# A hybrid attention/convolution block on one NeuronCore: x loaded in smaller first parts, its squares later, the warm-up on a zeroed tile, the transposes of q and k two half chunks later

## The chip, the cores and the metric

The kernel runs on one core of a Trainium2 chip. The metric is the device time of one execution in microseconds; the time before is the median of three runs. A profiled execution gives the trace that is read here; its clock starts at the program's first instruction, and its span ends with the last.

## What is computed

One layer for 256 tokens of width 2048, in float32 (the parts that matter here):

```python
xn = rms_norm(h, norm1_g[l])
proj = jnp.einsum('bsd,dn->bsn', xn, w_in[l])
q, k, v, ga, gg = jnp.split(proj, ...)
q = apply_rope(rms_norm(q, q_norm_g[l]), cos, sin)
k = apply_rope(rms_norm(k, k_norm_g[l]), cos, sin)
att = diff_attention(q, k, v, lam)          # 4 heads, block-causal mask
att = rms_norm(att, subln_g[l]) * (1.0 - lambda_init)
u = ga * jax.nn.sigmoid(gg)
u = causal_depthwise_conv(u, conv_w[l], conv_b[l])   # 31 taps
u = jax.nn.silu(layer_norm(u, conv_ln_g[l], conv_ln_b[l]))
h = h + jnp.einsum('bsm,md->bsd', jnp.concatenate([att, u], axis=-1), w_out[l])
hn = rms_norm(h, norm2_g[l])
a, bu = hn @ w_gate[l], hn @ w_up[l]
h = h + (jax.nn.silu(a) * bu) @ w_down[l]
```

## The kernel before

**Products in three passes.** Each operand of a large product is split into a high part (a cast, on ACT) and a low part (the rest, on DVE), and a product is high times high, low times high and high times low. The weights come in *chunks* of two 128-row tiles by 512 columns (512 KB). Of each chunk, `load_chunk` issues the transfer on SP (L315), `round_chunk` casts `whi` on ACT (L320), `split_chunk` makes `wlo` on DVE (L329), and `multiply` runs twelve matmuls: eight that read `whi` (L359, L360), then four that read `wlo` (L365). Five buffers hold raw chunks, three hold each of `whi` and `wlo`.

**The order is written out by hand.** `run_chunks` walks through the chunks. For chunk t it first issues the load, cast and split of chunk t+2 (t+1 in the opening, the first nine chunks), then chunk t's matmuls. All other work hangs on generators in the list `running`: `resume()` is called twice a chunk, after the first eight matmuls and after the last four, and lets each generator go on to its next `yield`. `lag(n)` waits for n such half chunks, `room` for free banks among the four `aux` banks of PSUM. What a generator issues goes into the engines' queues at that place, and each engine works through its queue in this order. Between these steps `run_side` gives DVE taps of the convolution (L517), as many as a credit allows.

**The opening.** A warm-up of 17 transposes of the identity matrix (L157) stands ahead of everything on PE; the identity and a small constant come from POOL. x arrives transposed, in parts: `XLOADS` says ahead of which chunk which of its 16 tiles are loaded (L433, into the buffers of q's and k's later transposes, `qT` and `kT`). `x_split` scales and casts each tile on ACT (L233) and makes the low part on DVE (L234). Chunks 0 and 1 hold one tile each, chunks 2 to 8 two. `x_norm` squares x in place in four parts of four tiles on ACT (L443), adds them on DVE (L445, L455), and sums over the partitions on PE (L460). It is started ahead of chunk 0, squares a part once its tiles are split, and one part a half chunk at most.

**The blocks of 512 columns.** The columns of `w_in` run in ten blocks: four of the convolution's gates (the first has nine chunks, the others eight), then k, q, k, q, then v twice. `qk_done` starts `qk_rows` for each half of the tokens (row 0, row 1), two half chunks apart. `qk_rows` sums squares on ACT (L427), takes the root on POOL (L217, L218, L615), after `LAG[0]` half chunks scales on ACT (L619), after `LAG[1]` rotates on DVE (L626 to L629), after `LAG[2]` transposes four tiles on PE (L634) and copies them on ACT (L635). When all rows of a k and a q block are there, `attend_scores` starts for two heads, four half chunks apart: scores on PE (L649), maxima on DVE (L657, L659), exponentials on ACT (L668), reciprocals on DVE and a factor on POOL (L677, L679), scaling on ACT (L688), sum on DVE (L695), transposes on PE (L701 to L703), copy on ACT (L706). `v_done` copies v on ACT (L712) and starts `attend_values` (PE L727), which waits for the copy of L706 and ends in transposes (L746) and the split of the result, from which the output projection reads. After that come the output projection, the gated feed-forward layer and the rest, which take the time from about 300 us to the end.

Of the kernel before, what the change touches and what calls it, by code (L numbers as in the profile page):

```python
# [12 lines left out]
F32 = mybir.dt.float32  # L13
# [5 lines left out]
P = 128  # L19
# [12 lines left out]
N = 512  # L32
# [17 lines left out]

WARM = 17

XLOADS = {0: range(0, 1), 1: range(1, 4), 3: range(4, 8), 5: range(8, 12), 7: range(12, 16)}
XSQUARES = 4

XWHOLE = 40
# [7 lines left out]
RAW_BUFS = 5  # L64
AUX = 4

LAG = (3, 2, 6)
HL_BUFS = 3

KTILE_US = 1.30  # L70
# [52 lines left out]
def tile_block(  # L123
# [6 lines left out]
    act, dve, pool, pe, sp = nc.scalar, nc.vector, nc.gpsimd, nc.tensor, nc.sync  # L130
# [8 lines left out]
    small = prestack.enter_context(tc.tile_pool(name="small", bufs=4))  # L139
    acc_ps = ctx.enter_context(tc.tile_pool(name="acc", bufs=4, space=PSUM))  # L140
    aux_ps = ctx.enter_context(tc.tile_pool(name="aux", bufs=AUX, space=PSUM))
# [3 lines left out]
    away = ctx.enter_context(tc.tile_pool(name="away", bufs=1, space=bass.MemoryType.DRAM))  # L145
    hd = [away.tile([P, D], F32, tag=f"hd{m}", name=f"hd{m}") for m in range(NM)]

    ident = const.tile([P, P], F32, tag="ident", name="ident")
    make_identity(nc, ident)
    neghalf = const.tile([P, 8], F32, tag="neghalf", name="neghalf")  # L150
    pool.memset(neghalf, -0.5)


    def warm_up(n):
        warm = aux_ps.tile([P, N], F32, tag="aux", name="ps_warm")
        for _ in range(n):
            pe.transpose(warm[:, :P], ident, ident)  # L157

    warm_up(WARM)

    cols = const.tile([P, NR], F32, tag="cols", name="cols")
    act.dma_start(out=cols, in_=gains)
# [78 lines left out]
    def start(gen):  # L241
        running.append(gen)
# [7 lines left out]
    def lag(n):  # L250
        for _ in range(n):
            yield
# [4 lines left out]
    def room(n, hold=0):  # L257
        while held[0] + n > AUX:
            yield
        held[0] += hold  # L260
# [170 lines left out]
    def x_load(ks):  # L431
        half = qkT["qk"[ks[0] // 8]]
        sp.dma_start(out=half[:, ks[0] % 8 : ks[-1] % 8 + 1, :], in_=xt[:, ks[0] : ks[-1] + 1, :])  # L433

    def x_split(ks):
        for k in ks:
            xT[k] = lhs_pair("x", k)
            split_scaled(xT[k], qkT["qk"[k // 8]][:, k % 8, :], col("g1", k))
# [8 lines left out]
    def x_norm():  # L447
        for n in range(KD // XSQUARES):
            while len(xT) < (n + 1) * XSQUARES:
                yield  # L450
            x_square(n)
            yield
        sq = qkT["q"]
        for w in (2, 1):
            dve.tensor_tensor(sq[:, :w, :], sq[:, :w, :], sq[:, w : 2 * w, :], ALU.add)  # L455
        yield from lag(2)
        yield from room(1)
        ps = aux_ps.tile([P, N], F32, tag="aux", name="ps_n")
        for m in range(NM):
            pe.matmul(ps[:, m : m + 1], sq[:, 0, m * P : (m + 1) * P], neghalf[:, :1], start=True, stop=True)  # L460
        yield
        ss = small.tile([P, NM], F32, tag="ss1", name="ss1")
        act.copy(ss, ps[:, :NM])
        for m in range(NM):
            rsqrt_mean(rstd1[m], ss[:, m : m + 1], -D / 2, EPS)
        yield
        normed.append(True)
# [138 lines left out]
    def qk_rows(key, b, m, ps):  # L606
# [8 lines left out]
        pool.tensor_scalar(f, f, rstd1[m], 0.0, ALU.mult, ALU.add)  # L615
        yield from lag(LAG[0])
        qn = pre.tile([P, G, DH], F32, tag="va", name="qn")
        for j in range(G):
            act.activation(qn[:, j, :], ps[:, j * DH : (j + 1) * DH], AF.Copy, scale=f[:, j : j + 1])  # L619
        yield from lag(LAG[1])  # L620
        t1 = pre.tile([P, G, DH], F32, tag="vb", name="t1")
# [7 lines left out]
        dve.tensor_tensor(t1, t1, t2, ALU.add)  # L629
        yield from lag(LAG[2])  # L630
        yield from room(1)
# [569 lines left out]
    def opening(i):  # L1201
        def begin():
            if i in XLOADS:
                x_load(XLOADS[i])
            x_split(chunks[i]["ks"])
            if not i:
                start(x_norm())
        return begin

# [37 lines left out]
```

## Time and profile before

| | |
|---|---|
| median of three runs | 1048.9 us (1048.76 to 1049.65) |
| the profiled execution | 1048.92 us |
| its span | 1047.1 us |
| TensorE matmuls, LDWEIGHTS | 4663 each |
| DMA | 231.30 MB, mean 221 GB/s |

In a timeline row, the first number is the start in us, the second the time, then the engine, the line of the kernel, the operation, the tiles written and read, and the count; in brackets stands how long the engine was idle before it and what ended that. A row with a count merges neighbours. PE is the matrix engine's matmuls and PEld its weight loads. A matmul's end is modelled and overlaps the next one's start, so the distance between starts is the better measure. In the table of stretches, the numbers are the stretch, its length, the busy time of PE, PEld, DVE, ACT and POOL with their instruction counts, the granted clock, the share of the DMA engines, and GB/s.

### The profile page before, as it was taken

How to read it: one execution, taken by the hardware profiler on the slowest of the kernel's cores; microseconds unless marked ns; L12 is line 12 of the kernel's file. 1: busy time of each engine (PE TensorE's matmuls, PEld its weight loads, DVE VectorE, ACT ScalarE, POOL GpSimd, SP SyncE). 2: the span in 40 equal slices, each digit the busy share in tenths (PEclk: the TensorE clock that was granted, in tenths of full speed). 3: DMA queues.
4: the chain of work that ended last, by engine and by line, in shares of the span. 5: the costliest groups of instructions: out<-in, count | busy, mean ns of one | idle time of the engine just before them, and what ended most of it. 6: DMA issues, size and time to landing. Idle time of an engine off the chain costs nothing.

```text
span 1047.1 us, 12933 instructions
## 1 busy us (share of the span) xinstructions
PE 1036.2 (99%) x4663; PEld 852.5 (81%) x4663; DVE 900.6 (86%) x1095; ACT 621.6 (59%) x786; POOL 100.5 (10%) x143
## 2 busy tenths in 40 slices
PE   9999999999999999999999999999999999999998
PEld 7888887877788788888888888888888888888886
DVE  7899889898765599999787898999878789989897
ACT  7544666755756565776463657666644446657442
POOL 0130122201100100000001010000000110000010
PEclk9999999999999999999999999999999999999999
DMA  9657654453546566987867789879757879798683
GB/s 335 227 182 280 212 163 167 154 181 134 177 153 226 194 223 214 268 266 236 232 210 188 217 271 273 256 217 285 248 175 241 219 208 291 222 287 267 187 265 85
DMA packets 113936, 231.30 MB, mean 221 GB/s; under 512 B 7504, under 2 KB 8656, under 8 KB 113616
## 3 DMA queue, kind: packets, MB, share of 16 engines
q1 hardware_dynamic: 104864, 203.71, 56.9%
q0 software_dynamic: 8864, 26.74, 13.4%
q8 instruction: 36, 0.59, 0.2%
q14 instruction: 28, 0.23, 0.1%
q10 hardware_dynamic: 144, 0.03, 0.0%
HBM read 204.24 MB, written 9.44 MB: 204 GB/s over the span
## 4 chain that ended last, share of the span: by engine, by line
PE 61%; DMA 2%; DVE 2%; issue 1%; ACT 0%; DVEq 0%; POOLq 0%
PE q L1020 12%; PE q L1014 12%; PE q L1015 12%; PE q L995 8%; PE q L993 7%; PE q L994 7%; DMA raw<-in_w_down_dram 1%; PE ps_a L831 1%; DMA wlo<-raw 1%; PE acc L365 1%; PE acc L359 1%; PE acc L360 1%; DVE wlo L329 1%; DVE wlt L976 0%; DVE wt L966 0%
## 5 line engine op out<-in xcount | busy, mean ns | idle before, releaser
L320 ACT CAST whi<-raw 128x1024 fp32r<-128x1024 f32 (+1 forms) x273 | 281.5, 1048 | 141.6 <-PE acc L360 58.9
L329 DVE TENSOR_TENSOR wlo<-raw,whi 128x1024 fp32r<-128x1024 f32 (+1 forms) x239 | 287.8, 1218 | 73.5 <-ACT whi L320 73.3
L972 ACT CAST wh<-wt 128x2048 fp32r<-128x2048 f32 x52 | 99.6, 1914 | 77.6 <-DVE wt L968 76.9
L976 DVE TENSOR_TENSOR wlt<-wt,wh 128x2048 fp32r<-128x2048 f32 x52 | 119.1, 2290 | 14.9 <-ACT wh L972 14.7
L359 PE MATMUL acc<-whi,xhi 128*128 128x512 f32 x320 | 126.9, 397 | 1.0 <-ACT whi L320 0.9
L360 PE MATMUL acc<-whi,xlo 128*128 128x512 f32 x320 | 125.2, 391 | 0.0
L1014 PE MATMUL q<-whi,chi 128*128 128x512 f32 x320 | 125.2, 391 | 0.0
L1015 PE MATMUL q<-whi,clo 128*128 128x512 f32 x320 | 124.5, 389 | 0.0
L993 PE MATMUL q<-wh,fhi 128*128 128x512 f32 x280 | 109.9, 393 | 0.0
L994 PE MATMUL q<-wh,flo 128*128 128x512 f32 x280 | 109.1, 390 | 0.0
L517 DVE SCALAR_TENSOR_TENSOR y<-upad,cw,y 128x256 f32<-128x256 f32 x240 | 102.2, 482 | 2.2 <-ACT y L510 2.2
L1014 PE MATMUL q<-whi,ahi 128*128 128x512 f32 x256 | 100.2, 391 | 0.0
L1015 PE MATMUL q<-whi,alo 128*128 128x512 f32 x256 | 99.6, 389 | 0.0
L975 DVE TENSOR_TENSOR wlb<-wb,wh 128x1536 fp32r<-128x1536 f32 x52 | 91.1, 1752 | 1.8 <-ACT wh L969 1.8
L365 PE MATMUL acc<-wlo,xhi 128*128 128x512 f32 x320 | 87.8, 396 | 2.0 <-DVE wlo L329 2.0
L1020 PE MATMUL q<-wlo,chi 128*128 128x512 f32 x320 | 85.7, 390 | 0.2 <-DMA wlo<-raw 0.2
L969 ACT CAST wh<-wb 128x1536 fp32r<-128x1536 f32 x52 | 76.6, 1474 | 0.0
L365 PEld LDWEIGHTS acc<-wlo,xhi 128*128 128x128 f32 x320 | 59.7, 189 | 15.3 <-DVE wlo L329 3.3
L359 PEld LDWEIGHTS acc<-whi,xhi 128*128 128x128 f32 x320 | 60.4, 189 | 14.3 <-ACT whi L320 1.9
L1020 PEld LDWEIGHTS q<-wlo,chi 128*128 128x128 f32 x320 | 59.9, 188 | 13.2 <-DMA wlo<-raw 0.8
L360 PEld LDWEIGHTS acc<-whi,xlo 128*128 128x128 f32 x320 | 60.4, 189 | 12.2
L1014 PEld LDWEIGHTS q<-whi,chi 128*128 128x128 f32 x320 | 60.1, 188 | 12.3
(230 smaller groups left out, 1739.1 us busy)
## 6 DMA issues: line engine op xcount, KB each, us to landing
raw<-in_w_in_dram SPq DMA_DIRECT2D x79, 512.0 KB, 4.6
raw<-in_w_down_dram SPq DMA_DIRECT2D x64, 512.0 KB, 7.2
raw<-in_w_gate_dram SPq DMA_DIRECT2D x48, 512.0 KB, 7.5
raw<-in_w_up_dram SPq DMA_DIRECT2D x48, 512.0 KB, 6.2
wb<-in_w_up_dram SPq DMA_DIRECT2D x40, 512.0 KB, 3.7
wb<-in_w_gate_dram SPq DMA_DIRECT2D x40, 512.0 KB, 4.9
wlo<-raw POOLq DMA_DIRECT2D x34, 512.0 KB, 7.1
raw<-in_w_out_dram SPq DMA_DIRECT2D x32, 512.0 KB, 4.2
```

What stands on the lines that cost most here:

```text
L320: act.copy(c["hi"], c["raw"])
L329: dve.tensor_tensor(c["lo"], c["raw"], c["hi"].bitcast(F32), ALU.subtract)
L359: pe.matmul(ps[m], xhi[:, ms], hi[:, j, :], start=c["first"] and j == 0, stop=False)
L360: pe.matmul(ps[m], xlo[:, ms], hi[:, j, :], start=False, stop=False)
L365: pe.matmul(ps[m], xhi[:, ms], lo[:, j, :], start=False, stop=c["last"] and j == nk - 1)
L517: dve.scalar_tensor_tensor(y[:, ct, :], src, wk, y[:, ct, :], ALU.mult, ALU.add)
L976: dve.tensor_tensor(lot, c["t"], c["hi"][:, :SUMMED].bitcast(F32), ALU.subtract)
L993: pe.matmul(ps, hi, c["hi"][:, w], start=bool(first), stop=False)
L994: pe.matmul(ps, lo, c["hi"][:, w], start=False, stop=False)
L1014: pe.matmul(ps, xs[i][0][:, ms], hi[:, i, :], start=i == 0 and bool(c["first"].get(qs[m])), stop=False)
L1015: pe.matmul(ps, xs[i][1][:, ms], hi[:, i, :], start=False, stop=False)
L1020: pe.matmul(sum_bank(c, qs[m]), xs[i][0][:, ms], lo[:, i, :], start=False, stop=i == 1 and bool(c["last"].get(qs[m])))
```

## The change

x's second part, which held three tiles ahead of chunk 1, becomes one tile ahead of chunk 1 and two ahead of chunk 2. `x_norm` starts ahead of chunk 4 in place of chunk 0. The warm-up's operand is a tile that DVE sets to zero, and its 17 products are plain matmuls in place of transposes. `LAG[2]` goes from 6 to 8.

```diff
-XLOADS = {0: range(0, 1), 1: range(1, 4), 3: range(4, 8), 5: range(8, 12), 7: range(12, 16)}
+XLOADS = {0: range(0, 1), 1: range(1, 2), 2: range(2, 4), 3: range(4, 8), 5: range(8, 12), 7: range(12, 16)}
+XSQUARED = 4
...
-LAG = (3, 2, 6)
+LAG = (3, 2, 8)
...
+    def warm_up(n):
+        zero = small.tile([P, P], F32, tag="zero", name="zero", bufs=1)
+        dve.memset(zero, 0.0)
+        warm = aux_ps.tile([P, N], F32, tag="aux", name="ps_warm")
+        for _ in range(n):
+            pe.matmul(warm[:, :P], zero, zero, start=True, stop=True)
+
+    warm_up(WARM)
+
     ident = const.tile([P, P], F32, tag="ident", name="ident")
     make_identity(nc, ident)
...
-
-    def warm_up(n):
-        warm = aux_ps.tile([P, N], F32, tag="aux", name="ps_warm")
-        for _ in range(n):
-            pe.transpose(warm[:, :P], ident, ident)
-
-    warm_up(WARM)
...
             x_split(chunks[i]["ks"])
-            if not i:
+            if i == XSQUARED:
                 start(x_norm())
```

## The prediction

> **What bounds the kernel now.** I read the page first, then the busy time in chosen stretches, then the timelines of each engine around every stretch in which PE is not full.
>
> ```profile
> span 1047.1 us, 12933 instructions
> PE 1036.2 (99%) x4663; PEld 852.5 (81%) x4663; DVE 900.6 (86%) x1095; ACT 621.6 (59%) x786; POOL 100.5 (10%) x143
> ```
>
> ```profile
> 0.00:10.00 10.00, 7.69 (x29) 6.39 (x29) 3.15 (x6) 5.32 (x9) 1.02 (x9) 1.00 0.75 249
> ...
> 142.00:167.00 25.00, 24.20 (x113) 19.81 (x112) 21.39 (x37) 16.07 (x38) 5.56 (x6) 1.00 0.42 136
> 167.00:192.00 25.00, 25.00 (x120) 20.86 (x119) 24.00 (x48) 19.38 (x55) 6.91 (x10) 1.00 0.52 180
> 192.00:219.00 27.00, 25.76 (x120) 20.68 (x119) 23.16 (x45) 17.81 (x41) 6.61 (x8) 1.00 0.53 175
> ...
> 245.00:268.00 23.00, 22.11 (x103) 17.62 (x103) 20.37 (x40) 12.72 (x27) 4.43 (x6) 1.00 0.56 190
> ```
>
> The columns behind the length of a stretch are PE, PEld, DVE, ACT and POOL busy time. PE sets the end: every idle microsecond of it is paid, and hardly anything else is. It lacks 2.3 us in the first ten, 0.8 in 142 to 167, 1.2 in 192 to 219 and 0.9 in 245 to 268. The change touches these places. The profiled execution took 1048.92 us (1.8 outside its span), the median of the three runs 1048.9; so I add to 1048.9.
>
> **The opening: warm-up, x, squares.**
>
> ```profile
> 0.73 0.21 POOL masks.py:197 MEMSET ident<- 128x128 f32 x1 [0.29 <-POOLq L1229]
> ...
> 1.36 3.89 PE L157 MATMUL ps_warm<-ident 128*128 128x128 f32 x17 [1.36 <-POOL neghalf L151]
> ...
> 2.11 0.92 SPq L315 DMA_DIRECT2D raw<-in_w_in_dram  x2
> ...
> 4.89 0.78 PE L359 MATMUL acc<-whi,xhi 128*128 128x512 f32 x1
> ...
> 5.47 0.63 PE L360 MATMUL acc<-whi,xlo 128*128 128x512 f32 x1
> ...
> 6.75 0.77 PE L365 MATMUL acc<-wlo,xhi 128*128 128x512 f32 x2
> ...
> 7.16 0.51 ACT L233 ACTIVATE xhi<-qT,cols 128x256 fp32r<-128x256 f32 x1 [2.54 <-DMA qT<-in_xt_dram]
> ...
> 9.13 1.04 ACT L320 CAST whi<-raw 128x1024 fp32r<-128x1024 f32 x1
> ...
> 10.22 0.19 PEld L359 LDWEIGHTS acc<-whi,xhi 128*128 128x128 f32 x1 [0.53 <-ACT whi L320]
> ...
> 14.96 1.06 ACT L443 ACTIVATE qT<-qT 128x1024 f32<-128x1024 f32 x1 [0.33 <-DVE xlo L234]
> ...
> 16.72 1.04 ACT L320 CAST whi<-raw 128x1024 fp32r<-128x1024 f32 x1
> ...
> 18.28 0.19 PEld L359 LDWEIGHTS acc<-whi,xhi 128*128 128x128 f32 x1
> ```
>
> ```profile
> raw<-in_w_in_dram SPq DMA_DIRECT2D x1, 512.0 KB, 6.5
> ```
>
> ```profile
> 170.77 1.47 PE L649 MATMUL ps_s<-kT,qT 128*128 128x128 f32 x8
> ...
> 190.29 1.08 PE L365 MATMUL acc<-wlo,xhi 128*128 128x512 f32 x4
> ```
>
> The warm-up moves from 17 transposes, one record each, to 17 plain float32 matmuls. Four plain float32 matmuls of L649 leave eight records, so 17 become 34. A transposing record starts (3.89 - 0.42) / 16 = 0.217 us after the last while the clock is low; real matmuls then start 0.43 apart (5.47 to 6.75 with two left out between). At full clock four start within 1.08 - 0.40 = 0.68, 0.227 apart (row at 190.29), and a chunk of twelve takes 2.72. The row from 170.77 has four records of 128 and four of 256 columns: at full clock 0.11 us for 128. So the warm-up grows from 3.5 us to 34 x 0.217 = 7.4 at the low clock. It starts after a memset like POOL's first one, at about 0.95 instead of 1.36. The pair from 6.75 takes 0.77, too little for two slow ones: the matmuls became fast at about 7.0, 5.7 after the warm-up began. If that comes after the same 5.7, 26 records run low and 8 at 0.11: the warm-up ends at 7.5. Chunks 0 and 1 follow at six matmuls each, 2 x 6 x 0.227 = 2.7: chunk 2 can start at 10.2. Today it starts at 10.22 after a wait for its cast (9.13), and that for its weights: the second issue of the pair at 2.11 starts near 2.6 and lands 6.5 later, at 9.1. The x pieces reorder the bytes ahead of that load and do not reduce them: chunk 1 gets its x earlier than 7.16, chunk 2 its weights no earlier. The one more issue costs SP about 0.45 (half of the 0.92 row), behind which SP's weight loads queue; the transfers are behind by 6.5 us, which hides it. So the gain up to chunk 2 is nothing, though before it PE waited; without the cover (chunk 1 late again) the old wait returns and still ends at 10.22. Bounds: a clock that rises only with the warm-up's end adds 0.8 us, to 8.3; a load that lands 1.2 us earlier lets chunk 2 start at 9.0 and gains 1.2, no more, as chunk 3 then waits for its own load. I take +0.1.
>
> The Trainium skill (TensorE: Matmul & The Clock Gate, Part 1) says that a busy window of about 3.4 us, free-running, lifts the clock. By it the rise falls between 4.4 and 7.8, the warm-up ends between 6.4 and 8.0, and the term is 0 to +0.5. Its Part 4 has transposes not count as busy; the trace speaks against that, since the clock rose 2.1 us after the first real matmul at 4.89, less than one window.
>
> The squares: the first one (1.06) leaves the place ahead of chunk 3's x and comes right before the second, behind chunk 4's cast. There 0.33 of idle time is used up; the cast for chunk 5 moves by 1.06 - 0.33 + small change, 0.6 to 0.7, from 16.72 to 17.4, and ends at 18.4. PE wants it at 18.28: +0.1. The DVE sum behind it moves as far; chunk 5's low parts keep slack. Opening: **+0.2** (-1.2 to +1.0).
>
> **The transposes two half chunks later.** I count half chunks as steps from a block's end. Rows 0 and 1 of a block put their transposes at steps 14 and 16 today, at 16 and 18 after. Step 16 is step 0 of the next block. ACT's copy (L635) of a transpose is a meeting with PE: ACT is ahead and waits there. Behind the meeting ACT has the next block's burst: squares at steps 3 and 5, scaling (L619) at 6 and 8.
>
> ```profile
> 142.63 0.59 ACT L635 COPY kT<-ps_qk 128x512 f32<-128x512 f32 x1 [2.56 <-PE ps_qk L634]
> ...
> 144.06 2.02 ACT L320 CAST whi<-raw 128x1024 fp32r<-128x1024 f32 x2
> 145.96 0.39 ACT L427 ACTIVATE junk<-acc,rstd 128x128 f32<-128x128 f32 x1
> ...
> 152.31 1.14 ACT L619 ACTIVATE qn<-acc,fq 128x128 f32<-128x128 f32 x4 [1.61 <-POOL fq L615]
> ```
>
> ```profile
> 148.50 3.40 POOL L218 TENSOR_TENSOR fq<-rsq,neghalf 128x4 f32<-128x4 f32 x1
> ```
>
> ```profile
> 154.42 1.23 DVE L329 TENSOR_TENSOR wlo<-raw,whi 128x1024 fp32r<-128x1024 f32 x1 [3.39 <-ACT whi L320]
> ...
> 163.47 1.22 DVE L329 TENSOR_TENSOR wlo<-raw,whi 128x1024 fp32r<-128x1024 f32 x1
> ```
>
> ```profile
> 141.99 0.60 PE L634 MATMUL ps_qk<-ident,t 128*128 128x128 f32 x4
> ...
> 161.49 0.60 PE L634 MATMUL ps_qk<-ident,t 128*128 128x128 f32 x4
> ...
> 164.74 1.20 PE L365 MATMUL acc<-wlo,xhi 128*128 128x512 f32 x4 [0.80 <-DVE wlo L329]
> ```
>
> *First q block's rows.* Today the last meeting (k, row 1) is at step 0, 142.63; two casts and the squares run on without a wait, to POOL's power of 3.40, the scaling at 152.31, a cast, and DVE, which had stood 3.39 us and is then busy to 164.69; PE waits 0.80. After, row 1's transposes stand at step 2, behind row 0's (four at 0.11) and one chunk of 2.72: at 141.99 + 0.44 + 2.72 = 145.15. The copy starts 0.64 behind them, as 142.63 does behind 141.99: 145.8, to 146.4. One of the two casts moves behind it, to 146.3 instead of 145.1. Everything after is +1.25, and DVE has no gap to make it up. On top, row 0's four transposes (161.49; 0.4) lie in front of PE's wait and shorten it today, and come behind it after. **+1.6** (0 if POOL's long power hides it, to 1.7).
>
> ```profile
> 177.16 0.69 DVE L659 TENSOR_REDUCE nmx<-ps_s 128x2 f32<-128x512 f32 x1
> 178.59 1.23 DVE L329 TENSOR_TENSOR wlo<-raw,whi 128x1024 fp32r<-128x1024 f32 x1 [0.73 <-ACT whi L320]
> ...
> 188.51 1.22 DVE L329 TENSOR_TENSOR wlo<-raw,whi 128x1024 fp32r<-128x1024 f32 x1
> ```
>
> *Second k block's rows.* The meeting comes at step 2 again, and the table load for the first exponentials moves from step 1 to step 3, from ahead of a cast to just ahead of the squares: the scaling, the cast and DVE's row at 178.59 come about 2.2 later. DVE is then busy to 189.73, 0.56 before PE wants it at 190.29. The first head's maxima (ending 177.85, in slack now) move into that stretch, the second head's out of it. 2.2 - 0.56 = **+1.6** (0 to 2.6, if the second head's maxima delay the chunk behind as well).
>
> ```profile
> 215.39 1.20 PE L365 MATMUL acc<-wlo,xhi 128*128 128x512 f32 x4 [1.24 <-DVE wlo L329]
> ```
>
> *Second q block's rows.* The same chain as the first, PE 1.24 behind DVE at its end. The same meeting gives **+1.3**; the first heads' probabilities, also two steps later, stand in ACT's queue ahead of the squares, which could make it 3.2; 0 below.
>
> ```profile
> 249.38 0.90 ACT L688 ACTIVATE p<-pr,a 128x128 f32<-128x128 f32 x2 [3.99 <-POOL a L679]
> ...
> 250.55 1.27 ACT L712 ACTIVATE v<-acc,rstd 128x512 f32<-128x512 f32 x2
> ```
>
> ```profile
> 251.29 1.56 PE L727 MATMUL ps_o<-v,qT 128*128 128x256 f32 x6 [0.28 <-ACT v L712]
> ...
> 258.33 0.91 PE L727 MATMUL ps_o<-v,qT 128*128 128x256 f32 x3 [0.57 <-ACT qT L706]
> ```
>
> *Heads 2 and 3.* Head 2's weights come two steps later, in the very step in which its values product (251.29) reads them; head 3's come one step later, as today its scores wait one step for free banks. So the product waits for a copy that directly follows its transposes, as head 3 does at 258.33: 0.57 against 0.28, +0.3. If ACT is as late as at 249.38, head 3's scaling (half a chunk later, +1.4), the copies of v and a cast of 1.0 stand ahead of that copy, itself about half a cast: 249.4 + 1.4 + 0.8 + 1.2 + 1.0 + 0.5 = 254.3 against 251.3, +3.0. I take **+1.5**.
>
> Sum: 0.2 + 1.6 + 1.6 + 1.3 + 1.5 = 6.2; 1048.9 + 6.2 = **1055.1 us**.
>
> **Rivals.** *POOL covers the meeting: not slower.* The scaling at 152.31 waits 1.61 for POOL. Today's squares end at 152.31 - 1.61 = 150.7. If the 3.40 power ends at a fixed time or turns out short, the squares end 1.25 later, at 152.0, and the scaling starts there, no later than today; likewise at the two later places. Then the four later terms are 0 to 0.3 and with the opening between -1.2 and +0.2 the time is 1047.7 to 1049.4. It decides as long as POOL's result is there before 152.3. Against it: POOL's chain begins with the end of the first squares, which move. *Only the first place pays:* ACT and DVE make good the rest during PE's new wait: 1048.9 + 0.2 + 1.6 = 1050.7. Against it: each meeting is set by PE's own position, so a wait of PE gives ACT nothing. *Zeros do not lift the clock:* the warm-up ends at 8.3, chunks 0 and 1 run at 0.43 a matmul, 5.1 us, chunk 2 starts at 13.4 instead of 10.2: +3.1 on the sum, 1058.2. For it, the profile shows no matmul on zeros; against it, transposes of an identity, mostly zeros, do so now. *The warm-up's length is not doubled* (one record each): 1055.0, as the loads hold chunk 2.
>
> **How the numbers follow.** Forecast 0.65, POOL cover 0.15, only the first place 0.12, cold clock 0.08. 0.2% is 2.1 us, about what a measurement of this kernel can tell from no change. The forecast's own range takes the four later terms between low and middle (1.9) and near their high ends (9): 1051 to 1058.5. To leave out no more than two in ten, the low end goes down to 1050, which takes in the first place alone; the cover and part of the cold clock stay out: 1050 to 1058.5. Faster needs the cover with its opening gain and another gain not seen here, 0.08; same takes most of the cover and some of the first place alone, 0.14; slower has 0.78.
>
> **What would show it.** Right: plain warm-up matmuls to about 7.5 in 34 records, chunk 2 starting near 10.2; ACT's copy of row 1 about 2.7 us into the next block, DVE's long idle before its low parts 1.2 us later against PE than today, and PE's waits for wlo at the four places about 2.5, 1.6, 2.7 and 2 us. Wrong: PE as busy there as now, or chunk 2 a microsecond off 10.2. A copy at which ACT hardly waits would overturn the middle of the argument.

## The result, and the profile after

The changed kernel takes 1062.53 us (median of four runs, 1062.0 to 1063.38); beside it the kernel before took 1049.18 us (1048.76 to 1049.65). The ratio is 1.0128 (95% interval 1.011 to 1.0145): slower, by about 13.4 us where 6.2 were forecast, and outside the range. A line from L161 of the kernel before on has a number 3 higher in the changed kernel; the warm-up's product moves from L157 to L154.

First the page of the changed kernel, span and busy time, then its table of stretches (columns as in the prediction).

```profile
span 1061.6 us, 12966 instructions
PE 1042.6 (98%) x4680; PEld 857.0 (81%) x4680; DVE 901.3 (85%) x1096; ACT 623.2 (59%) x786; POOL 102.9 (10%) x143
```

```profile
142.00:167.00 25.00, 23.84 (x112) 19.42 (x110) 21.52 (x39) 15.63 (x36) 4.66 (x6) 1.00 0.41 132
...
192.00:219.00 27.00, 24.58 (x110) 18.65 (x108) 21.06 (x42) 19.33 (x49) 7.79 (x10) 1.00 0.43 138
219.00:245.00 26.00, 20.48 (x102) 16.87 (x101) 23.75 (x46) 12.95 (x30) 2.19 (x4) 1.00 0.48 161
245.00:268.00 23.00, 21.77 (x90) 17.69 (x91) 18.60 (x41) 13.35 (x30) 5.33 (x6) 0.93 0.41 137
```

The kernel before had, from 219 on, in its table:

```profile
219.00:245.00 26.00, 26.00 (x124) 21.79 (x123) 24.49 (x51) 17.30 (x44) 2.49 (x6) 1.00 0.36 124
```

In this stretch, where PE was full before, the PE of the changed kernel lacks 5.5 us, and its next stretch has a granted clock of 0.93. Busy time can mislead here: a matmul at half clock counts as busy. The waits stand in the timeline of PE:

```profile
1.04 6.63 PE L154 MATMUL ps_warm<-zero 128*128 128x128 f32 x34 [1.04 <-DVE zero L151]
7.42 0.47 PE L362 MATMUL acc<-whi,xhi 128*128 128x512 f32 x1
...
11.08 0.50 PE L362 MATMUL acc<-whi,xhi 128*128 128x512 f32 x1 [0.66 <-ACT whi L323]
...
165.55 1.21 PE L368 MATMUL acc<-wlo,xhi 128*128 128x512 f32 x4 [1.16 <-DVE wlo L332]
...
191.57 1.19 PE L368 MATMUL acc<-wlo,xhi 128*128 128x512 f32 x4 [0.27 <-DVE wlo L332]
...
198.29 0.50 PE L362 MATMUL acc<-whi,xhi 128*128 128x512 f32 x1 [1.49 <-ACT whi L323]
...
211.17 0.50 PE L362 MATMUL acc<-whi,xhi 128*128 128x512 f32 x1 [0.80 <-ACT whi L323]
...
220.68 1.19 PE L368 MATMUL acc<-wlo,xhi 128*128 128x512 f32 x4 [1.66 <-DVE wlo L332]
...
240.81 0.67 PE L749 MATMUL ps_at<-ident,att 128*128 128x128 f32 x4 [0.84 <-DVE malo L237]
241.31 0.61 PE L652 MATMUL ps_s<-kT,qT 128*128 128x128 f32 x4
244.94 1.61 PE L652 MATMUL ps_s<-kT,qT 128*128 128x256 f32 x4 [3.02 <-DVE malo L237]
...
263.80 1.56 PE L730 MATMUL ps_o<-v,qT 128*128 128x256 f32 x6 [1.23 <-ACT qT L709]
...
298.61 0.49 PE L362 MATMUL acc<-whi,mchi 128*128 128x512 f32 x1 [1.70 <-DVE mchi L585]
```

The kernel before had 0.80 at the first q rows, 1.24 at the second, 0.28 and 0.57 at the values products, and, in its timeline of PE, this for `mchi`:

```profile
286.20 0.50 PE L359 MATMUL acc<-whi,mchi 128*128 128x512 f32 x1 [0.58 <-DVE mchi L582]
```

Against these the timeline names 0.9 us in the opening (11.08 against 10.22), 0.4 at 165, 0.3 + 1.5 + 0.8 between 191 and 212, 0.4 at 220, 3.9 at 240 to 245, 0.4 at 264 and 1.1 at 299: 9.7 of the 14.5 us between the two spans (1061.6 against 1047.1). At 165 the wait is 1.16 for 0.80, since the four transposes that used to run ahead of it (0.4) now run behind it. The second big piece is the clock. In this table of stretches of the changed kernel the column after POOL is the granted clock:

```profile
241.97:245.39 3.42, 0.45 (x2) 0.45 (x3) 2.88 (x6) 1.80 (x9) 0.00 (x0) 1.00 0.00 0
245.39:248.80 3.41, 3.41 (x10) 2.66 (x9) 2.23 (x6) 1.44 (x4) 0.00 (x0) 0.50 0.00 0
248.80:252.21 3.41, 3.41 (x16) 2.75 (x16) 3.31 (x10) 1.46 (x2) 0.93 (x2) 1.00 0.39 118
296.59:300.00 3.41, 1.71 (x8) 1.06 (x7) 2.69 (x6) 3.03 (x5) 0.00 (x0) 1.00 0.32 100
300.00:303.41 3.41, 3.41 (x12) 2.71 (x11) 1.10 (x2) 0.82 (x2) 0.00 (x0) 0.50 0.14 53
```

Twice PE runs at half clock for 3.41 us, each time right behind a stretch in which it stood: at most 1.7 us each. With them 13.1 of the 14.5 have a row. The rest lies between the rows: since a matmul's modelled end reaches past the next one's start, a wait shows less idle time than it adds between starts (the one at 191.57 shows 0.27, but lies 0.66 behind the start before it, where 0.23 is usual). Counted by the start of the same chunk in both timelines, nothing is left over. The changed kernel is behind by 0.93 us at 29.75 (times of the kernel before), 1.33 at 185.27, 5.26 at 208.76, 5.76 at 229.03, 11.59 at 245.04, 11.74 at 279.12 and 14.49 at 298.37.

**What stands behind the two largest waits.** Near 197 us, in the timelines of ACT, POOL and DVE:

```profile
193.66 0.40 ACT L691 ACTIVATE p<-pr,a 128x128 f32<-128x128 f32 x1 [6.66 <-POOL a L682]
195.19 0.51 ACT L691 ACTIVATE p<-pr,a 128x256 f32<-128x256 f32 x1 [1.12 <-POOL a L682]
...
197.19 1.05 ACT L323 CAST whi<-raw 128x1024 fp32r<-128x1024 f32 x1
```

```profile
193.22 1.94 POOL L682 TENSOR_TENSOR a<-r,neg_lam 128x1 f32<-128x1 f32 x2 [13.39 <-DVE r L680]
```

```profile
192.98 0.22 DVE L680 RECIPROCAL r<-sm 128x2 f32<-128x2 f32 x2
```

ACT stands 6.66 us for head 0's factor, which hangs on DVE's reciprocal at 192.98. Behind it in ACT's queue are the exponentials of head 1 and then the cast (197.19) for which PE stands at 198.29. Near 241 us it is DVE:

```profile
240.58 1.66 DVE L520 SCALAR_TENSOR_TENSOR y<-upad,cw,y 128x256 f32<-128x256 f32 x4
242.15 1.22 DVE L332 TENSOR_TENSOR wlo<-raw,whi 128x1024 fp32r<-128x1024 f32 x1
243.29 0.48 DVE L237 SCALAR_TENSOR_TENSOR malo<-ps_at,cols,mahi 128x256 fp32r<-128x256 f32 x1
244.31 0.48 DVE L237 SCALAR_TENSOR_TENSOR malo<-ps_at,cols,mahi 128x256 fp32r<-128x256 f32 x1 [0.54 <-ACT mahi L236]
```

The scores of head 3 need two of the four `aux` banks. The first is free (241.31). The second is granted when the last `malo` of head 1 has been read (244.31 + 0.48 = 244.79; PE goes on at 244.94): it is the bank into which PE transposed head 1's result at 240.81, half a microsecond earlier. `room` lets this pass, since its count holds the banks of scores and of values products, and not a bank of transposes that ACT and DVE have yet to read. In which half of which chunk PE takes these pieces up, from the order of its matmuls (chunks counted from 0; a: behind the first eight of the chunk, b: behind its last four):

```
                           before   changed   first block only (b2)   second block only (b3)
head 3's scores             76b      77a           76b                     77a
head 1's ps_at              77a      77a           77a                     77a
convolution's ps_y, 2nd     88a      88b           88a                     88b
```

### The profile page after: what moved, and what is told of

It is laid out like the page before. It is cut to its first block, busy times and chain, and to the rows that moved or that the text cites. A ratio compares the mean times of both kernels' runs of the same rounds, so it can differ in the third digit from the quotient of the medians.

```text
span 1061.6 us, 12966 instructions
## 1 busy us (share of the span) xinstructions
PE 1042.6 (98%) x4680; PEld 857.0 (81%) x4680; DVE 901.3 (85%) x1096; ACT 623.2 (59%) x786; POOL 102.9 (10%) x143
## 4 chain that ended last, share of the span: by engine, by line
PE 57%; DVE 3%; DMA 2%; issue 1%; ACT 1%; SPq 0%; DVEq 0%; POOLq 0%
PE q L1023 11%; PE q L1017 11%; PE q L1018 11%; PE q L998 7%; PE q L996 7%; PE q L997 7%; DVE wlo L332 1%; DMA raw<-in_w_gate_dram 1%; DMA raw<-in_w_down_dram 1%; PE ps_a L834 1%; PE acc L368 1%; PE acc L363 1%; PE acc L362 1%; ACT wh L975 1%; DVE wt L969 1%
## 5 line engine op out<-in xcount | busy, mean ns | idle before, releaser
L323 ACT CAST whi<-raw 128x1024 fp32r<-128x1024 f32 (+1 forms) x273 | 282.2, 1050 | 152.4 <-PE acc L363 62.0
L979 DVE TENSOR_TENSOR wlt<-wt,wh 128x2048 fp32r<-128x2048 f32 x52 | 119.1, 2290 | 14.5 <-ACT wh L975 14.3
L1023 PEld LDWEIGHTS q<-wlo,chi 128*128 128x128 f32 x320 | 59.9, 188 | 13.4 <-DMA wlo<-raw 0.9
L1018 PEld LDWEIGHTS q<-whi,clo 128*128 128x128 f32 x320 | 60.1, 188 | 12.3
```

The costliest lines, as they stand in the source:

```text
L323: act.copy(c["hi"], c["raw"])
L979: dve.tensor_tensor(lot, c["t"], c["hi"][:, :SUMMED].bitcast(F32), ALU.subtract)
L1018: pe.matmul(ps, xs[i][1][:, ms], hi[:, i, :], start=False, stop=False)
L1023: pe.matmul(sum_bank(c, qs[m]), xs[i][0][:, ms], lo[:, i, :], start=False, stop=i == 1 and bool(c["last"].get(qs[m])))
```

## The experiments

### The lag or the opening; head 3 moved away

**a1** is the kernel before with the new lag alone, **a2** the changed kernel with the old lag, so the opening alone. **a3** and **a4** start head 3 later.

```diff
-LAG = (3, 2, 6)                    # a1, in the kernel before
+LAG = (3, 2, 8)
...
-LAG = (3, 2, 8)                    # a2, in the changed kernel
+LAG = (3, 2, 6)
...
-                yield from lag(4)  # in qk_done, in the changed kernel
+                yield from lag(4 + 2 * b)   # a3
+                yield from lag(4 + b)       # a4
```

> The kernel before with the later transposes alone (lag 8 for 6); the opening is that of before. Theory A (the lag pays nearly all, the opening about 0.9 of the 13.6 us): 1061.0 to 1062.5 us, PE waits about 3 us for head 3's scores near 241 us, and the granted clock shows a stretch at half near 245 us. Rival B (the opening's late loads and the lag work together, the one alone does little): below 1058 us.

> The changed kernel with the transposes back at lag 6: x parts, squares and warm-up alone. Theory A: 0.9 us over before at chunk 2, and it stays: 1049.8 to 1050.4 us, no stretch at half clock behind the warm-up. Rival B: a lateness of 0.9 us that upsets the head scaling as well: 1053 us or more.

> The changed kernel, but head 3 starts six half chunks behind head 2 instead of four, so that its scores come one step behind head 2's exponentials. Theory A (its scores stop PE because the four spare PSUM banks are two of head 2's scores and two that ACT and DVE are still reading): the wait of 3.2 us near 241 us and the half clock near 245 us are gone, lag at chunk 78 about 5 us instead of 11.6: 1055.5 to 1058.5 us. Rival C (ACT and DVE are simply behind there, and PE meets them at the next product anyway): the wait comes back within four chunks at another instruction, 1061 us or more.

> The changed kernel, but head 3 starts five half chunks behind head 2: its scores come in the very step of head 2's exponentials, as in the kernel before. Theory A, if the bank they take is one of those exponentials' or of a transpose read a step earlier: a wait of 0 to 1.5 us instead of 3.2, no half clock, 1055.5 to 1059 us. Rival C: 1061 us or more.

| | median, us | ratio to before (95%) |
|---|---|---|
| before, same chip | 1048.55 | |
| a1 | 1059.67 | 1.0107 (1.0093 to 1.012) |
| a2 | 1048.58 | 1.0003 (0.9994 to 1.0011) |
| a3 | 1058.95 | 1.0101 (1.0087 to 1.0114) |
| a4 | 1058.41 | 1.0098 (1.0083 to 1.0113) |

The lag pays, and the opening pays nothing; theory A had 0.9 us there. The row that moved chunk 2 is ACT's cast, one row each of a2, of the changed kernel (the same opening) and of a1 (the opening of before, in which the profiled execution had 9.13):

```profile
9.47 1.05 ACT L323 CAST whi<-raw 128x1024 fp32r<-128x1024 f32 x1 [0.43 <-DMA raw<-in_w_in_dram]
```

```profile
9.98 1.05 ACT L323 CAST whi<-raw 128x1024 fp32r<-128x1024 f32 x1 [0.43 <-DMA raw<-in_w_in_dram]
```

```profile
9.51 1.04 ACT L320 CAST whi<-raw 128x1024 fp32r<-128x1024 f32 x1 [1.12 <-DMA raw<-in_w_in_dram]
```

The landing of the same load moves by 0.5 us between executions with one and the same opening, so about half of the 0.9 read off one trace was such a shift.

a1 is a little short of A's range: its profiled execution has one half clock where the changed kernel has two. PE's wait for the scores in a3, then in a4:

```profile
244.77 1.10 PE L652 MATMUL ps_s<-kT,qT 128*128 128x256 f32 x4 [0.29 <-DVE malo L237]
```

```profile
243.32 1.10 PE L652 MATMUL ps_s<-kT,qT 128*128 128x256 f32 x4 [2.09 <-DVE malo L237]
```

In a3 it shrinks from 3.02 to 0.29 us, as A said, and the half clock near 245 us goes (another, near 296, stays); the 0.84 at `ps_at` remains. In a4, with the scores one step later, it is 2.09, more than the 0 to 1.5 expected, yet there is no half clock. By the ratios both are about 3 us faster than the changed kernel; a4 lies inside A's range and a3 0.45 us above it. That is less than the wait and the half clock together. Part of the lateness comes back, as rival C had it: by the starts of the chunks a3 is 4.6 us ahead of the changed kernel at 245 (times of the kernel before) and 3.5 at 279. But C's 1061 us falls.

### The heads or the transposes; which block; the half clock

**b1** keeps the transposes where they were and starts only the heads two half chunks later; it tells the forecast's mechanism (ACT's copy meeting PE early in the next block) from the heads' own lateness. **b2** and **b3** give the new lag to one block's rows alone. **b4** puts twelve small products of zeros into the running sum ahead of head 3's scores, so that PE has something to do while it waits.

```diff
             while not all((k, b, m) in placed for k in "qk" for m in range(NM)):
                 yield
+            yield from lag(2)                               # b1, in the kernel before
...
-        yield from lag(LAG[2])                              # b2, b3, in the kernel before
+        yield from lag(LAG[2] + 2 * (b == 0))               # b3: b == 1
...
         yield from room(2, 2)                               # b4, in the changed kernel
+        if hd == 3:
+            for _ in range(FILL):                        # FILL is 12
+                pe.matmul(current[0][1][:, :P], zero[0], zero[0], start=False, stop=False)
```

> The kernel before, transposes at lag 6, but each pair of heads starts two half chunks later, as in the changed kernel; ACT's copies of the transposes stay at steps 0 and earlier. Theory A (what costs is the heads' work, met by the next block's burst two half chunks later, and at last the bank clash of head 3's scores): 1057 to 1061 us, with PE's waits near 197, 210, 219 and 241 us as with the later transposes alone. Rival D (the prediction's: ACT's copies meeting PE at step 2 cost): 1049 to 1051 us.

> The kernel before with lag 8 for the rows of the first k and q block alone: heads 0 and 1 come two half chunks later, heads 2 and 3 as before. Theory A: the waits near 197, 210 and 219 us are there (about 4 us together); head 3's scores come a step after head 2's exponentials' neighbours of before, with no wait of 3 us: 1052 to 1055 us. Rival D: three of its four terms lie at these rows and the next block's: about 1050 us, all of it behind the first q block.

> The kernel before with lag 8 for the rows of the second k and q block alone: heads 2 and 3 come two half chunks later, heads 0 and 1 as before. Theory A: nothing ahead of 215 us; head 3's scores and the chunks behind cost between 0 and 5 us, more if they still ask for banks that are being read: 1049 to 1054 us. Rival D: the term of the second q block and that of heads 2 and 3, 2.8 us: 1051.5 us.

> The changed kernel with twelve small matmuls on zeros (24 records of 0.11 us) added to the running sum right ahead of head 3's scores, where PE stands 3.2 us. Theory E (the half clock of 3.41 us near 245 us follows from PE standing in the 3.41 us before it): no half clock there, the wait for the banks shrinks from 3.2 to about 0.5 us of standing, head 3's scores start when they did, and the time falls by 1.5 us or a little more: 1060 to 1061.2 us. Rival F (the low clock is set by something else, or the added matmuls delay the scores): 1062.3 us or more.

| | median, us | ratio to before (95%) | half clocks in the profiled execution |
|---|---|---|---|
| before, same chip | 1048.24 | | none |
| b1 | 1059.02 | 1.0100 (1.0085 to 1.0115) | 3 |
| b2 | 1052.65 | 1.0042 (1.0027 to 1.0057) | 1 |
| b3 | 1056.92 | 1.0082 (1.0065 to 1.0099) | 2 |
| b4 | 1058.89 | 1.0101 (1.0086 to 1.0116) | none |

b1 costs about as much as the whole lag (1.0107), with not one copy at a later place. So by these ratios the meeting on which the forecast rested costs nothing that can be told from zero, and the heads' lateness costs nearly all. What the transposes' own move costs shows in the timelines of PE, at the last wait for `wlo` of each q block: 1.16 and 1.70 us in a1 against 0.79 and 1.10 in b1 (0.80 and 1.24 in the kernel before). b2's loss is one wait and the half clock behind it, in its timeline of PE:

```profile
197.49 0.79 PE L359 MATMUL acc<-whi,xhi 128*128 128x512 f32 x1 [1.93 <-ACT whi L320]
```

The waits that A expected near 210 and 219 us did not come in b2, nor the one near 210 in b1. The one near 219 goes with the second block's transposes (1.24 in b2, as before; 1.71 in b3). The loss behind the one near 210 came all the same: between the chunks that start at 185 and at 209 us (times of the kernel before) b1 and b2 lose 4.1 us, 1.7 of it to a half clock, and the changed kernel and a1, without a half clock there, 3.9. b3 has what is left, in its timeline of PE:

```profile
235.41 0.67 PE L746 MATMUL ps_at<-ident,att 128*128 128x128 f32 x4 [0.81 <-DVE malo L234]
...
239.54 2.05 PE L649 MATMUL ps_s<-kT,qT 128*128 128x256 f32 x4 [3.03 <-DVE malo L234]
...
293.64 0.49 PE L359 MATMUL acc<-whi,mchi 128*128 128x512 f32 x1 [1.69 <-DVE mchi L582]
```

It cost more than either theory had for it (A up to 1054, "more if they still ask for banks that are being read", which they did). Heads 2 and 3 alone bring the bank clash and the later `mchi`. In b4 the stretch that PE stood through is filled, and the clock stays up; its table of stretches:

```profile
241.40:244.80 3.40, 3.06 (x27) 2.90 (x27) 2.86 (x7) 1.78 (x8) 0.00 (x0) 1.00 0.00 0
244.80:248.20 3.40, 3.40 (x16) 2.83 (x16) 3.35 (x8) 1.71 (x5) 0.00 (x0) 1.00 0.02 5
```

Head 3's scores go on at 244.63, after a wait of 0.34 us, as early as without the filler. The time falls by 2.8 us by the ratios (3.6 between the medians), more than theory E's 1.5, and ends below its range: both half clocks are gone, since the wait for `mchi` (1.69 here too) now falls on two stretches of the 3.41 us grid, 1.48 of it in one (last section). Rival F falls.

### Three repairs, and a shorter lag

**c1** lets ACT scale the second softmax half a chunk later, so that it doesn't stand for POOL ahead of the cast. **c2** lets the layer norm scale half a chunk earlier. **c3** is the changed kernel with lag 4. **c4** is c1, c2 and a3 together.

```diff
-        yield from lag(2)          # c1: ahead of p
+        yield from lag(3)
         p1s = []
...
-        yield from lag(2)          # c1: ahead of the weights
+        yield from lag(1)
         wts = []
...
-        yield from lag(2)          # c2: in conv_back, ahead of the scaling
+        yield from lag(1)
...
-LAG = (3, 2, 8)                    # c3
+LAG = (3, 2, 4)
```

> The changed kernel, but ACT's scaling of the second softmax (p) comes half a chunk later and the weights after it as late as now. Theory A (near 197 us ACT stands for POOL's factor, which waits for DVE's reciprocal, and the cast that PE needs is queued behind it): PE's wait of about 1.5 us there goes to under 0.4 us and the one near 211 us shrinks too: 1059.5 to 1061.5 us. Rival G (the casts are late for the casts' own order, not for p): the wait near 197 us stays, 1062 us or more.

> The changed kernel with the layer norm's scaling of the convolution half a chunk earlier, so that its transposes stand between a chunk's halves, as in the kernel before. Theory A (PE's wait of 1.7 us for mchi and the half clock right behind it come of the half chunk that this step had slipped): wait about 0.6 us as before, no half clock near 300 us: 1059.5 to 1061.5 us. Rival G (POOL's factors are the last to come, so an earlier place gains nothing): 1062 us or more.

> The changed kernel's opening with lag 4: transposes and heads two half chunks earlier than before. Theory A (what counts is where the heads' work meets the bursts and the banks; lag 6 lies between, so the other side is open): 1046 to 1056 us; it gains only if the waits near 165 and 215 us (0.8 and 1.24 us) shrink. Rival D (later transposes only add lateness at ACT's copies): earlier ones gain 0 to 1 us, 1047.5 to 1048.5 us.

> The changed kernel with the three repairs together: p half a chunk later, the layer norm half a chunk earlier, head 3 two half chunks later. Theory A (three separate causes, each with its wait, and half clocks that follow from two of them): 1052.5 to 1056 us, no half clock before the end. Rival C (the lateness moves on to the next product): 1058 us or more.

| | median, us | ratio to before (95%) |
|---|---|---|
| before, same chip | 1048.48 | |
| c1 | 1057.97 | 1.0089 (1.0075 to 1.0103) |
| c2 | 1061.07 | 1.0121 (1.0107 to 1.0135) |
| c3 | 1047.31 | 0.9987 (0.9978 to 0.9996) |
| c4 | 1055.53 | 1.0063 (1.0049 to 1.0077) |

c1 gains more than expected, 4 us by the ratios: its timeline of PE has no wait between 191 and 217 us, and the profiled execution has one half clock instead of two. ACT takes the exponentials and the cast (193.37 for 197.19) first, and then doesn't wait for POOL at all:

```profile
193.37 1.04 ACT L323 CAST whi<-raw 128x1024 fp32r<-128x1024 f32 x1
194.31 0.81 ACT L691 ACTIVATE p<-pr,a 128x128 f32<-128x128 f32 x2
```

This trace alone does not settle it. POOL's two factors, which took 1.94 us in the changed kernel, took 0.81 in it; in a4, without c1's edit, they took 0.80, and PE's wait near 197 us is 0.36 there for 1.49. But d2 (below) has c1's edit with factors of 1.94, and its PE has no wait there either.

c2 missed. Its time lies within A's range by the number, but without the shorter wait that was to give it:

```profile
299.43 0.50 PE L362 MATMUL acc<-whi,mchi 128*128 128x512 f32 x1 [1.90 <-DVE mchi L585]
```

c4 lands inside A's range, without any half clock, with `mchi` still at 1.90. c3 shows the other side of the edge: with the heads two half chunks *earlier* than before, PE is full where the kernel before waited 0.80, by its table of stretches:

```profile
142.00:167.00 25.00, 25.00 (x120) 20.81 (x119) 22.65 (x40) 17.15 (x39) 4.77 (x6) 1.00 0.45 147
```

It is the fastest of all these kernels, ahead of the one before by 0.13% (0.04 to 0.22), less than the 0.2% that I had set as a difference to be told. Its time lies in A's wide range and 0.2 us below rival D's.

### The late `mchi`

What c2 left open: the layer norm comes late because its chain begins late (`ps_y` in 88b for 88a in the table above), or because POOL and ACT are late. **d1** starts that chain half a chunk earlier, **d2** adds c1 and a3 to it, **d3** is lag 5, and **e1** is lag 5 with d1.

```diff
-        yield from lag(3)          # d1, d2, e1: first line of conv_back's waiting
+        yield from lag(3 - b)
...
-LAG = (3, 2, 8)                    # d3, e1
+LAG = (3, 2, 5)
```

> The changed kernel, but the second convolution half's way back begins half a chunk earlier, so that its first transposes (ps_y) and with them the whole chain up to the layer norm stand where they did before. Theory A2 (the late step is the beginning of that chain, not its scaling): PE's wait for mchi falls from 1.7 to about 0.6 us and no half clock follows it: 1059.5 to 1061.3 us. Rival G2 (the layer norm is late because POOL or ACT are late): the wait stays at 1.7 us, 1061.5 us or more.

> The changed kernel with p half a chunk later, head 3 two half chunks later and the way back of the convolution half a chunk earlier. Theory A2: as the three repairs of before (1055.5 us), less the 1.1 us at mchi: 1053.5 to 1055.3 us. Rival C: 1055.5 us or more.

> The changed kernel's opening with lag 5, one half chunk before the kernel before. Theory A2 (each wait is a matter of which step's burst the heads' work falls in): between lag 4 (1047.3 us) and lag 6 (1048.6 us) if nothing collides, 1047 to 1049 us. Rival H (odd steps put the work into the other half of each chunk, where casts and not low parts are queued): 1050 us or more.

> The changed kernel with lag 5 and the second half's way back of the convolution half a chunk earlier. Theory A2 (with lag 5 only the slipped chain up to mchi pays, 1.69 us of waiting for 0.58): 1.1 us under lag 5 alone, 1048.3 to 1048.9 us, about the kernel before. Rival G2 (the lateness comes back further on): 1049.5 us or more.

| | median, us | before, same chip | ratio (95%) |
|---|---|---|---|
| d1 | 1059.05 | 1048.37 | 1.0104 (1.009 to 1.0117) |
| d2 | 1053.22 | 1048.37 | 1.0046 (1.0032 to 1.0059) |
| d3 | 1049.7 | 1048.37 | 1.0016 (1.0007 to 1.0025) |
| e1 | 1048.38 | 1048.36 | 1.0000 (0.9991 to 1.0009) |

In d1's timeline of PE the wait is what it was before the change:

```profile
296.77 0.50 PE L362 MATMUL acc<-whi,mchi 128*128 128x512 f32 x1 [0.58 <-DVE mchi L585]
```

So A2 holds: the chain begins late. d1 gains 2.5 us by the ratios, which puts it 0.45 us below A2's range: 1.1 at this row and up to 1.7 by the half clock that no longer follows. e1 tells it without a half clock. Lag 5 alone (d3) has this as its one large wait, and so came out above A2's range, though below rival H's 1050:

```profile
286.82 0.50 PE L362 MATMUL acc<-whi,mchi 128*128 128x512 f32 x1 [1.69 <-DVE mchi L585]
```

The same edit there gives 1.3 us (1.7 by the ratios) and the time of before. d2, with all three causes undone, is a little faster than expected and leaves 4.9 of the 13.4 us. By the starts of its chunks they lie in many places: 0.2 us in the opening, 0.4 up to 185 (times of the kernel before), 1.3 up to 209, 0.5 up to 229, 1.5 up to 245 and 1.2 up to 279. The time does not grow evenly with the lag: 4, 5, 6 and 8 half chunks give 0.9987, 1.0016, 1.0003 and 1.0128.

## Why the prediction was wrong

The sign, and the place of the changed kernel's trouble from 190 us on, were right; the mechanism and so the size were not.

- **Opening, +0.2.** Right within the noise: ratio 1.0003. The warm-up has 34 records from 1.04 and chunk 0 follows at 7.42 (7.5 forecast). Zeros lift the clock: chunk 0's first matmul takes 0.47 us, for 0.78 before. Chunk 2 at 11.08 instead of 10.2 looked like a miss, but the same opening in a2 lands it half a microsecond earlier.
- **First q block's rows, +1.6: the step that failed.** The forecast wrote that everything behind the meeting is "+1.25, and DVE has no gap to make it up", and carried this on as a term at the next two places. The meeting came, but POOL took it up. Changed kernel, ACT, then POOL:

```profile
146.24 0.59 ACT L638 COPY kT<-ps_qk 128x512 f32<-128x512 f32 x1 [0.66 <-PE ps_qk L637]
...
153.11 1.15 ACT L622 ACTIVATE qn<-acc,fq 128x128 f32<-128x128 f32 x4 [0.69 <-POOL fq L618]
```

```profile
149.70 0.94 POOL L220 TENSOR_SCALAR rsq<-ssq 128x4 f32<-128x4 f32 x1 [20.52 <-ACT junk L430]
150.73 1.98 POOL L221 TENSOR_TENSOR fq<-rsq,neghalf 128x4 f32<-128x4 f32 x1
```

  The copy comes where it was forecast (145.8 and the opening's shift), and still stands 0.66 for PE. POOL's power, which took 3.40 when it began at 148.50, takes 1.98 when it begins at 150.73. The scaling starts 0.80 later (153.11 against 152.31), no more than the 0.9 that this execution had lost in the opening. That is the rival "POOL covers the meeting", at this place. Of the 1.6 only the 0.4 came that the forecast had put on top, for the four transposes that no longer run ahead of PE's wait. b1, which has nearly all the loss and no such meeting, shows that the meeting explains little at the other places too.
- **Second k block's rows, +1.6.** PE's wait for `wlo` there was 0.27. What cost 1.5 and 0.8 us next to it (about 4 us by the starts of the chunks, 1.33 to 5.26) was another thing: head 0's scaling, standing in ACT's queue for POOL ahead of a cast. The forecast counted the head's maxima on DVE here; the first heads' probabilities in ACT's queue it named only one block later, as an upper bound. c1 and d2 show it.
- **Second q block's rows, +1.3.** 0.4 (1.66 for 1.24), which comes with the transposes (a1, b3) and not with the heads (b1).
- **Heads 2 and 3, +1.5.** At the values product 0.4, by the forecast's own mechanism. The forecast was also right that head 3 comes "one step later, as today its scores wait one step for free banks": its scores go from 76b to 77a, its transposed weights from 84a to 84b. But it did not ask who holds the banks in that step: `room` no longer makes the scores wait, and so they take a bank that is still being read. This is the largest wait of all, 3.0 us, and it takes the clock down with it.
- **Not in the forecast:** the half clocks (up to 1.7 us each, two in the profiled execution) and the late `mchi` (1.1). The prediction read the clock only in the opening.

The cold-clock rival fell with the warm-up, "only the first place pays" had the wrong place. What stays open: why exactly the convolution's chain starts half a chunk later with the later heads, why POOL's power was shorter, and what causes the 4.9 us that d2 still loses.

## What to carry to other kernels

When a step with a tail of dependent work is moved, follow the tail and not the step: here the transposes' own move cost about 0.4 us at each of two waits, and nearly all the loss lay in what started behind them, some of it at the far end of that tail. Look at what an in-order queue puts behind an instruction that waits for a slow small engine, and at whether a bank counted as free has been read. On a PE that is nearly always busy, a wait of some 2 us can cost nearly 4, so fill it or split it.

## What the hardware showed

**Half a stretch of standing takes the clock down.** With the traces of all these kernels cut into stretches of 3.413 us from the first change to full clock, and the ends apart, where PE has run out of work, each of the 15 stretches at half clock follows one in which PE stood for 1.69 us or more; of the stretches with full clock behind them the longest standing is 1.70 us (one of 1.80 in the last 6 us of a2 apart). So in these traces the edge lies at about 1.70 us, half the stretch. It is the sum in a stretch that counts, and not the length of a wait. In a4 waits of 0.81 and 2.09 us fall for the most part on two stretches evenly (1.37 and 1.36), and nothing follows:

```profile
238.54:241.96 3.42, 2.05 (x12) 1.69 (x12) 3.41 (x7) 2.02 (x4) 0.00 (x0) 1.00 0.01 5
241.96:245.37 3.41, 2.05 (x9) 1.80 (x10) 2.87 (x8) 3.02 (x10) 0.00 (x0) 1.00 0.00 0
245.37:248.78 3.41, 3.41 (x16) 2.80 (x16) 3.31 (x10) 1.76 (x3) 0.34 (x2) 1.00 0.22 67
```

In the changed kernel 1.70 us near 298 are enough (its row 296.59:300.00 above). So one and the same wait costs 1.7 us more or not by where it falls. The times of these kernels scatter by up to 3 us (a1: 1057.8 to 1060.84, the kernel before beside it 1047.7 to 1049.09); how much of that is the clock is not shown. The Trainium skill (TensorE: Matmul & The Clock Gate, Part 1) has a free-running window of 3413 ns. The trace agrees: the two half clocks of the changed kernel begin 54.61 us apart (245.39 and 300.00), which is 16 such windows.

**POOL's small operations have no fixed price.** The 128x4 power of the first q block's row 0 took 3.40 us in the four traces in which the first block's transposes have lag 6 (the kernel before, a2, b1, b3), 1.98 to 2.01 in the eleven with lag 8 there, and 1.27 to 1.30 in the three with lag 4 or 5. It is not the time of its start: it took 3.40 from 148.93 on in a2 and 1.27 from 149.06 on in c3. Nor does it end at a fixed time (149.4 to 153.0 us). Head 0's two factors took 1.94 us in the changed kernel and 0.80 in a4, with the same code up to there. What sets these times is not shown.
